# Masks, head products and the attention gate: two shared PSUM banks, and the gate's silu moved into attention

## The chip, the cores and the metric
The kernel runs on one core of a Trainium2 chip. TensorE (PE) does the matmuls into PSUM, of which there are eight banks of 128 x 512 float32; VectorE (DVE), ScalarE (ACT) and GpSimd (POOL) read and write SBUF and, but for POOL here, PSUM; SyncE (SP) issues the DMAs. Each engine runs its own instructions in order, and semaphores make one wait for another. The metric is the device time of one execution in microseconds; lower is better.

## The reference
An encoder layer over 1536 tokens: a prompt of 512 (seq0) and a sequence of 1024 (seq1). After a normed and modulated input, one in-projection feeds a latent attention branch and a bidirectional state space (SSD) branch, which are gated and projected out. What matters here is the SSD over chunks of 128 tokens, in 4 groups of 8 heads of width 64, both directions, and the attention's output gate:

```python
CB = einsum('bclgn,bcsgn->bcgls', Cc, Bc)            # one product of B and C per chunk and group
y_diag = einsum('bcgls,bcgels,bcsgep->bclgep', CB, Lm, xdt)   # Lm: decays, masked to one triangle
y_off  = einsum('bclgn,bcgepn,bclge->bclgep', Cc, prev, exp(a_cum))
y = y_diag + y_off + D * x                            # forward; the backward pass is summed to it
...
attn = softmax(q k^T) v * silu(gate_a)                # per head of 128
```

The exact form of the rest (norms, rotary part, convolution of width 5, projections) does not change.

## The kernel before
Tokens are worked on in windows of 512 (W), the SSD in chunks of 128 (P): 4 of seq0, 8 of seq1. A matmul of full precision is three products of split operands (mm3, L88 to L90). The stages follow one another: input and modulation to about 85 us, the four SSM groups to about 1600, attention to about 2190, then the output projections.

In each group g the convolution blocks of B, C and x come first, then `prepass` (the states of the backward direction, which are written out) and `mainpass` for seq0 and seq1. The program is written as generators: at every step of `mainpass` or `prepass` some blocks of the in-projection are fed in between as filler for PE (the 'mm' products). Groups 0 and 1 have the gate's eight blocks among their filler: two in group 0, six in group 1, three windows each. Their evacuation is a tanh on ACT (L524), (tanh + 1) times x on DVE (L525) and a store to `sgA` (L526). A scheduler places instructions by the program's order and its pools; semaphores are set by itself, and pools give out slots in turn.

`mainpass` takes a chunk in two halves of four heads (u = 0 and 1). By name: `head` (transposes through PSUM slots "sm", the copy `xb`, the product of B and C at L651 and its two masked forms `cu` at L653 and L654), `distances` (the load of `ab`), `weights` (POOL's differences L714, ACT's scaled masks `t` and `wt` at L718 and L719, DVE's sum L720, predicated copy L721, ACT's exponential L722), `weigh` (L727), `products` (four head matmuls into `py`, L738; the profile counts them in halves), `state` (`bth`, `btl`, `zt`: L688 to L691), `follow` (the new state, mm3 and DVE's `stf`), `carried` (what the old states give: matmuls L677 with `stf` and `sb`, DVE L678, sum L680) and `tail` (the sum of `py`, L743, and into x, L744). PSUM: three banks "mm" for the projections, three "sm" that transposes, the product of B and C, states and carried products share in turn, and two for `py`.

In attention a unit is one head and one window. `scores` makes the four blocks of scores and exponentials, `values` multiplies with v, and `gates` loads the gate `gt` (L1042), multiplies it by the softmax's reciprocal on POOL (L1043), and DVE applies it (L1072). 24 units; their steps are merged by weights, so that one unit's scores stand beside the one before's values.

Of the kernel before, what the change touches and what calls it, by code (L numbers as in the profile page):

```python
# [9 lines left out]
F32 = mybir.dt.float32  # L10
F32R = mybir.dt.float32r
U8 = mybir.dt.uint8
AF = mybir.ActivationFunctionType
ALU = mybir.AluOpType
AX = mybir.AxisListType
PSUM = bass.MemoryType.PSUM
DRAM = bass.MemoryType.DRAM

P = 128
T = 1536  # L20
W = 512
# [44 lines left out]
def _body(nc, tc, A, O):  # L66
    V, S, GP, PE = nc.vector, nc.scalar, nc.gpsimd, nc.tensor
    pools = []

    def pool(name, bufs=1, space=None, side="left"):  # L70
        cm = tc.tile_pool(name=name, bufs=bufs, side=side) if space is None else tc.tile_pool(name=name, bufs=bufs, space=space)
        p = cm.__enter__()
        pools.append((name, cm))
        return p
# [29 lines left out]
    cmat = const.tile([P, 5, P], F32, name="cmat")  # L104
    nc.sync.dma_start(out=cmat, in_=A["cmat"])
    maskb = const.tile([P, P], U8, name="maskb")
    ident, triF, triB, selL, selF = (cmat[:, i, :] for i in range(5))
# [153 lines left out]
    close("p0")  # L261


    yp = pool("yp", bufs=2, space=PSUM)
    p1 = pool("p1")
    pS = pool("pb", side="right")

# [246 lines left out]
    def filler(kind, i):  # L514
        if kind == "qc":
            def ev(w, ps):
                t = tmp("ft")
                S.copy(t, ps)
                nc.sync.dma_start(out=qcT[i][w], in_=t)
            return inproj_steps(i, ev)  # L520
        elif kind == "gate":
            def ev(w, ps):
                t = tmp("ft")
                S.activation(t, ps, AF.Tanh, scale=0.5)  # L524
                V.scalar_tensor_tensor(t, t, 1.0, ps, op0=ALU.add, op1=ALU.mult)  # L525
                nc.sync.dma_start(out=sgA[i][w], in_=t)  # L526
            return inproj_steps(BLK_GATE + i, ev)
        else:
            dst = tga if kind == "ga" else tgb

            def ev(w, ps):
                t = tmp("ft")
                S.activation(t, ps, AF.Tanh, scale=0.5)
                nc.sync.dma_start(out=dst[i][w], in_=t)
            return inproj_steps((BLK_GA if kind == "ga" else BLK_GB) + i, ev)
# [34 lines left out]
    for g in range(G):  # L570
# [61 lines left out]
        def mainpass(o, n):  # L632
# [5 lines left out]
            def head(c):  # L638
                cs_ = slice(c * P, (c + 1) * P)
                if c == c0:  # L640
                    xb = tok(c, "xb", 2)
                else:
                    xb = pS.tile([P, W + P], F32, name="xb", bufs=2)
                    nc.sync.dma_start(out=xb, in_=xbD[g][c])
                xt, bt = xb[:, :W], xb[:, W:]
                sb = None
                if c < c1 - 1:
                    sb = pS.tile([P, W], F32, name="sb", bufs=2)
                    nc.sync.dma_start(out=sb, in_=sbD[g][c])
                pc = smp.tile([P, P], F32, name="sm")  # L650
                PE.matmul(pc, lhsT=Bt[:, cs_], rhs=Ct[:, cs_], start=True, stop=True)  # L651
                cu = pS.tile([P, 2, P], F32, name="cu", bufs=2)
                V.tensor_tensor(cu[:, 0, :], pc, triF, op=ALU.mult)  # L653
                V.tensor_tensor(cu[:, 1, :], pc, triB, op=ALU.mult)  # L654
                stt[c] = dict(xt=xt, bt=bt, sb=sb, cu=cu)

            def decays(c):
                eb = {}
# [35 lines left out]
            def follow(c):  # L694
                stt[c]["sf"] = sf[0]
                if c < c1 - 1:
                    ps = smp.tile([P, W], F32, name="sm")
                    mm3(ps, *stt[c]["parts"], True, True)
                    sf[0] = advance(sf[0], ps, 0, c, pS.tile([P, W], F32, name="stf", bufs=2))
# [25 lines left out]
            def weigh(c, u):  # L725
                ab, wt = stt[c, u]
                V.tensor_tensor(wt, ab[:, 0], wt, op=ALU.mult)  # L727
                stt[c, u] = wt

            def products(c, u):  # L730
                e0 = u * HH
                wt = stt.pop((c, u))
                if u == 0:
                    stt[c]["py"] = yp.tile([P, 4, P], F32, name="py")
                py = stt[c]["py"]
                for e in range(e0, e0 + HH):
                    j = e % 2
                    PE.matmul(py[j * 64:j * 64 + 64, e // 2, :], lhsT=stt[c]["xt"][:, e * 64:e * 64 + 64], rhs=wt[:, e - e0, :], start=True, stop=True)  # L738

            def tail(c):  # L740
                cs_ = slice(c * P, (c + 1) * P)
                off = stt[c]["off"]
                V.tensor_tensor(off, off, stt[c]["py"], op=ALU.add)  # L743
                V.tensor_tensor(xa[:, :, cs_], xa[:, :, cs_], off, op=ALU.add)  # L744

            nu = E // HH
            us = [(c, u) for c in range(c0, c1) for u in range(nu)]
            head(c0)
            for i in range(4):
                xo = xs[i][:, o:o + n]  # L750
# [3 lines left out]
            weights(*us[0])  # L754
            yield
            for i in range(len(us) + 1):
                if i < len(us):
                    weigh(*us[i])
                if i + 2 < len(us):
                    distances(*us[i + 2])  # L760
                if i >= 1:
                    products(*us[i - 1])
                if i < len(us) and us[i][1] == 1:
                    follow(us[i][0])
                    carried(us[i][0])
                if i >= 1 and us[i - 1][1] == nu - 1:
                    tail(us[i - 1][0])
                if i + 1 < len(us):
                    weights(*us[i + 1])
                if i < len(us) and us[i][1] == 0:  # L770
                    c = us[i][0]
                    state(c)
                    decays(c)
                    if c + 1 < c1:
                        head(c + 1)
                yield
# [194 lines left out]
    def scores(u):  # L971
# [31 lines left out]
        def block(b):  # L1003
# [21 lines left out]
                S.activation(pp[k], sps[k], AF.Exp, bias=sm[:, 2:3], scale=rq[:, b, h:h + 1], accum_out=st["su"][:, k, b:b + 1])  # L1025
            PT[u].append(pp)

        def gates():

            su = st["su"]  # L1030
            if nw == 2:
                V.tensor_tensor(su[:, 0], su[:, 0], su[:, 1], op=ALU.add)
            V.reciprocal(su[:, 0], su[:, 0])
            pt = spp.tile([4, P], F32, name="sp")
            PE.transpose(out=pt, in_=su[:, 0], identity=ident)
            rt = p2.tile([4, P], F32, name="rt", bufs=2)
            S.copy(rt, pt)
            nc.sync.dma_start(out=rsD[hd][o // W + w].rearrange("(b q) -> b q", b=4), in_=rt)
            rb = p2.tile([P, W], F32, name="rb", bufs=1)
            nc.sync.dma_start(out=rb, in_=rsD[hd][o // W + w].partition_broadcast(P))  # L1040
            gt = p2.tile([P, W], F32, name="gt", bufs=1)
            nc.sync.dma_start(out=gt, in_=sgA[hd][o // W + w])  # L1042
            GP.tensor_tensor(gt, gt, rb, op=ALU.mult)  # L1043
            GT[u] = gt

        GT[u] = gates
        return [turn_n, turn_r], [lambda b=b: block(b) for b in range(4)]

    def values(u):

# [217 lines left out]
```

## Time and profile before

| | |
|---|---|
| median of 3 runs | 2720.13 us (2719.35 to 2723.41) |
| the profiled execution | 2716.42 us, span 2714.4, 2.0 us around it |
| mean granted clock of PE | 0.985 of full speed |
| busy: PE, DVE, ACT, POOL | 2586.5, 1833.5, 1322.6, 505.1 us |
| busy share of the same | 95%, 68%, 49%, 19% |

The busy share of PE is an average over stages with different limits; what holds a stage up is read from the waits and the timeline of that stage. A row of the waits says which tile's instruction waited, and the last operation that it waited for. A timeline row carries the idle time of its engine just ahead of it, with the releaser, in brackets. [...]

### The profile page before, as it was taken

What the parts mean: (1) busy time and instruction counts of PE and PEld (TensorE: products, weight loads), DVE (VectorE), ACT (ScalarE), POOL (GpSimd) and SP (SyncE); (2) the same over time, 40 slices, a digit from 0 to 9 for tenths busy, and PEclk for the clock granted to TensorE, in tenths of its full rate; (3) what the DMA queues carried; (4) which work ended last, traced back from release to release, by engine and by line L of the source; (5) the groups of instructions that cost most, each with busy time, mean ns of one, the idle gap of its engine ahead of it and who ended that gap; (6) DMA issues with size and microseconds to landing.
All of it is one profiled execution on the core that took longest, in us unless ns stands there. A gap on an engine that the chain in (4) does not pass through costs nothing. (4 is left out here: it accounts for less than half of the span.)

```text
span 2714.4 us, 36314 instructions
## 1 busy us (share of the span) xinstructions
PE 2586.5 (95%) x12810; PEld 2080.5 (77%) x12810; DVE 1833.5 (68%) x2962; ACT 1322.6 (49%) x2954; POOL 505.1 (19%) x455
## 2 busy tenths in 40 slices
PE   6999999999999998999998999999999999999999
PEld 2776777877778766878766888888888788888887
DVE  5878785788946678557777568877777753466631
ACT  5545654456624456564556357666665651111210
POOL 1013440023400035110135024322222200000000
PEclk8999999999999999999999999999999999999999
DMA  7227662156722266542466322211110252255433
GB/s 249 77 78 208 187 168 94 39 179 187 207 62 86 82 208 183 136 147 74 146 191 188 92 96 87 84 44 43 34 40 28 71 186 70 78 156 163 128 125 101
DMA packets 211205, 325.86 MB, mean 120 GB/s; under 512 B 24816, under 2 KB 74064, under 8 KB 210256
## 3 DMA queue, kind: packets, MB, share of 16 engines
q1 hardware_dynamic: 211024, 323.55, 39.9%
q8 instruction: 101, 1.65, 0.3%
q14 instruction: 80, 0.66, 0.1%
HBM read 245.56 MB, written 77.91 MB: 119 GB/s over the span
## 5 line engine op out<-in xcount | busy, mean ns | idle before, releaser
L88 PE MATMUL mm<-hH,wh 128*128 128x512 f32 x1656 | 670.2, 405 | 2.3 <-ACT hH L218 2.0
L89 PE MATMUL mm<-hL,wh 128*128 128x512 f32 x1656 | 662.0, 400 | 3.6 <-DVE hL L219 3.6
L90 PE MATMUL mm<-hH,wl 128*128 128x512 f32 x1656 | 653.7, 395 | 1.3 <-DVE wl L85 1.2
L88 PEld LDWEIGHTS mm<-hH,wh 128*128 128x128 f32 x1656 | 314.6, 190 | 84.6 <-issue 14.6
L89 PEld LDWEIGHTS mm<-hL,wh 128*128 128x128 f32 x1656 | 315.4, 190 | 77.3 <-issue 10.2
L90 PEld LDWEIGHTS mm<-hH,wl 128*128 128x128 f32 x1656 | 314.6, 190 | 73.2 <-issue 6.1
L714 POOL TENSOR_TENSOR ab<-ab,dg 128x512 f32<-128x512 f32 x192 | 236.9, 1246 | 418.5 <-DMA ab<-arD 293.4
L88 PE MATMUL mm<-hi,wh 128*128 128x512 f32 x768 | 298.8, 389 | 0.0
L90 PE MATMUL mm<-hi,wl 128*128 128x512 f32 x768 | 298.8, 389 | 0.0
L89 PE MATMUL mm<-lo,wh 128*128 128x512 f32 x768 | 298.8, 389 | 0.0
L85 DVE TENSOR_TENSOR wl<-ws,wh 128x512 fp32r<-128x512 f32 x210 | 151.3, 722 | 134.4 <-ACT wh L226 86.7
L361 ACT CAST wh<-ws 128x512 fp32r<-128x512 f32 x72 | 44.9, 623 | 326.4 <-PE mm L89 311.3
L88 PEld LDWEIGHTS mm<-hi,wh 128*128 128x128 f32 x768 | 144.1, 188 | 30.1
L89 PEld LDWEIGHTS mm<-lo,wh 128*128 128x128 f32 x768 | 144.1, 188 | 29.9
L90 PEld LDWEIGHTS mm<-hi,wl 128*128 128x128 f32 x768 | 144.1, 188 | 29.9
L719 ACT ACTIVATE wt<-cu,dg 128x128 f32<-128x128 f32 x384 | 141.3, 391 | 46.5 <-DVE cu L653 46.1
L1025 ACT ACTIVATE pp<-sp,smx,rq 128x512 f32<-128x512 f32 x160 | 123.6, 777 | 54.9 <-DVE smx L1020 38.8
L361 ACT CAST ph<-tp 128x512 fp32r<-128x512 f32 x160 | 95.3, 598 | 110.4 <-PE tp L1059 110.2
L689 POOL TENSOR_TENSOR btl<-xb,bth 128x128 fp32r<-128x128 f32 x40 | 28.5, 713 | 607.5 <-ACT bth L688 607.4
L563 DVE SCALAR_TENSOR_TENSOR xs<-raw,cwh,xs 128x511 f32<-128x511 f32 (+3 forms) x128 | 129.7, 1021 | 17.5 <-ACT xs L559 14.8
L718 ACT ACTIVATE t<-cu,dg 128x128 f32<-128x128 f32 x384 | 137.3, 390 | 2.6 <-DVE cu L654 2.4
L721 DVE COPY_PREDICATED ab<-maskb,ab 128x512 f32<-128x512 uint8 x96 | 86.4, 905 | 69.3 <-POOL ab L714 69.3
(293 smaller groups left out, 5018.5 us busy)
## 6 DMA issues: line engine op xcount, KB each, us to landing
ab<-arD SPq DMA_DIRECT2D x192, 256.0 KB
ws<-w_in SPq DMA_DIRECT2D x140, 256.0 KB
eb<-arD SPq DMA_DIRECT2D x160, 128.0 KB
xbD<-xp SPq DMA_DIRECT2D x40, 320.0 KB
xb<-xbD SPq DMA_DIRECT2D x40, 320.0 KB
yT<-xs SPq DMA_DIRECT2D x48, 256.0 KB
sg<-yT SPq DMA_DIRECT2D x48, 256.0 KB
tg<-tga SPq DMA_DIRECT2D x48, 256.0 KB
```

The source lines that it names most:

```text
L85: V.tensor_tensor(out, a, b, op=ALU.subtract)
L88: PE.matmul(out, lhsT=ah, rhs=bh, start=first, stop=False)
L89: PE.matmul(out, lhsT=ah, rhs=bl, start=False, stop=False)
L90: PE.matmul(out, lhsT=al, rhs=bh, start=False, stop=last)
L361: S.copy(hi, src)
L563: V.scalar_tensor_tensor(acc[:, lo:hi], raw[:, lo + d:hi + d], cwh[:, 24 + 24 * k + tix:24 + 24 * k + tix + 1], acc[:, lo:hi], op0=ALU.mul ...
L689: GP.tensor_tensor(bl, stt[c]["bt"], r32(bh), op=ALU.subtract)
L714: GP.tensor_tensor(ab[:, d], ab[:, d], ac_[:, d, c, e0:e0 + HH].unsqueeze(2).broadcast_to([P, HH, P]), op=ALU.subtract)
L718: S.activation(t1[:, e], cu[:, 1, :], AF.Copy, scale=dt_[:, 1, c, e0 + e:e0 + e + 1])
L719: S.activation(wt[:, e], cu[:, 0, :], AF.Copy, scale=dt_[:, 0, c, e0 + e:e0 + e + 1])
L721: V.copy_predicated(ab[:, 0], maskb.unsqueeze(1).broadcast_to([P, HH, P]), ab[:, 1])
L1025: S.activation(pp[k], sps[k], AF.Exp, bias=sm[:, 2:3], scale=rq[:, b, h:h + 1], accum_out=st["su"][:, k, b:b + 1])
```

## The change
The product of B and C gets a bank of its own (`pcb`), in which chunk c writes quarter c mod 4, and is made by a function `masks` one chunk ahead, at the start of a chunk; both masked forms are one DVE operation of 128 x 256. The heads' products of both halves get one bank (`pyb`) for all chunks; each half is summed into the carried part by a function `total` of its own, straight behind the carried products, and `tail` keeps only the sum into x. `state` stands at the start of a chunk's first half, ahead of `weigh`. The gate's evacuation becomes a plain copy, and tanh (ACT) and two products (POOL) go to attention, into a step `silu` behind the four score blocks of each unit; the gate has three buffers, the tanh one.

```diff
--- before.py
+++ after.py
@@ -261,7 +261,9 @@
     close("p0")
 
 
-    yp = pool("yp", bufs=2, space=PSUM)
+    yp = pool("yp", space=PSUM)
+    pyb = yp.tile([P, 4, P], F32, name="py")
+    pcb = yp.tile([P, 4, P], F32, name="pc")
     p1 = pool("p1")
     pS = pool("pb", side="right")
 
@@ -521,8 +523,7 @@
         elif kind == "gate":
             def ev(w, ps):
                 t = tmp("ft")
-                S.activation(t, ps, AF.Tanh, scale=0.5)
-                V.scalar_tensor_tensor(t, t, 1.0, ps, op0=ALU.add, op1=ALU.mult)
+                S.copy(t, ps)
                 nc.sync.dma_start(out=sgA[i][w], in_=t)
             return inproj_steps(BLK_GATE + i, ev)
         else:
@@ -647,12 +648,16 @@
                 if c < c1 - 1:
                     sb = pS.tile([P, W], F32, name="sb", bufs=2)
                     nc.sync.dma_start(out=sb, in_=sbD[g][c])
-                pc = smp.tile([P, P], F32, name="sm")
+                stt[c] = dict(xt=xt, bt=bt, sb=sb, cu=stt[c])
+
+            def masks(c):
+
+                cs_ = slice(c * P, (c + 1) * P)
+                pc = pcb[:, c % 4, :]
                 PE.matmul(pc, lhsT=Bt[:, cs_], rhs=Ct[:, cs_], start=True, stop=True)
                 cu = pS.tile([P, 2, P], F32, name="cu", bufs=2)
-                V.tensor_tensor(cu[:, 0, :], pc, triF, op=ALU.mult)
-                V.tensor_tensor(cu[:, 1, :], pc, triB, op=ALU.mult)
-                stt[c] = dict(xt=xt, bt=bt, sb=sb, cu=cu)
+                V.tensor_tensor(cu, pc.unsqueeze(1).broadcast_to([P, 2, P]), cmat[:, 1:3, :], op=ALU.mult)
+                stt[c] = cu
 
             def decays(c):
                 eb = {}
@@ -730,21 +735,21 @@
             def products(c, u):
                 e0 = u * HH
                 wt = stt.pop((c, u))
-                if u == 0:
-                    stt[c]["py"] = yp.tile([P, 4, P], F32, name="py")
-                py = stt[c]["py"]
                 for e in range(e0, e0 + HH):
                     j = e % 2
-                    PE.matmul(py[j * 64:j * 64 + 64, e // 2, :], lhsT=stt[c]["xt"][:, e * 64:e * 64 + 64], rhs=wt[:, e - e0, :], start=True, stop=True)
+                    PE.matmul(pyb[j * 64:j * 64 + 64, e // 2, :], lhsT=stt[c]["xt"][:, e * 64:e * 64 + 64], rhs=wt[:, e - e0, :], start=True, stop=True)
+
+            def total(c, u):
+                off = stt[c]["off"][:, 2 * u:2 * u + 2, :]
+                V.tensor_tensor(off, off, pyb[:, 2 * u:2 * u + 2, :], op=ALU.add)
 
             def tail(c):
                 cs_ = slice(c * P, (c + 1) * P)
-                off = stt[c]["off"]
-                V.tensor_tensor(off, off, stt[c]["py"], op=ALU.add)
-                V.tensor_tensor(xa[:, :, cs_], xa[:, :, cs_], off, op=ALU.add)
+                V.tensor_tensor(xa[:, :, cs_], xa[:, :, cs_], stt[c]["off"], op=ALU.add)
 
             nu = E // HH
             us = [(c, u) for c in range(c0, c1) for u in range(nu)]
+            masks(c0)
             head(c0)
             for i in range(4):
                 xo = xs[i][:, o:o + n]
@@ -754,22 +759,28 @@
             weights(*us[0])
             yield
             for i in range(len(us) + 1):
+                c, u = us[min(i, len(us) - 1)]
+                begins = i < len(us) and u == 0
+                if begins:
+                    if c + 1 < c1:
+                        masks(c + 1)
+                    state(c)
                 if i < len(us):
-                    weigh(*us[i])
+                    weigh(c, u)
                 if i + 2 < len(us):
                     distances(*us[i + 2])
                 if i >= 1:
                     products(*us[i - 1])
-                if i < len(us) and us[i][1] == 1:
-                    follow(us[i][0])
-                    carried(us[i][0])
+                if i < len(us) and u == 1:
+                    follow(c)
+                    carried(c)
+                if i >= 1:
+                    total(*us[i - 1])
                 if i >= 1 and us[i - 1][1] == nu - 1:
                     tail(us[i - 1][0])
                 if i + 1 < len(us):
                     weights(*us[i + 1])
-                if i < len(us) and us[i][1] == 0:
-                    c = us[i][0]
-                    state(c)
+                if begins:
                     decays(c)
                     if c + 1 < c1:
                         head(c + 1)
@@ -1025,6 +1036,15 @@
                 S.activation(pp[k], sps[k], AF.Exp, bias=sm[:, 2:3], scale=rq[:, b, h:h + 1], accum_out=st["su"][:, k, b:b + 1])
             PT[u].append(pp)
 
+        def silu():
+
+            gt = st["gt"] = p2.tile([P, W], F32, name="gt", bufs=3)
+            nc.sync.dma_start(out=gt, in_=sgA[hd][o // W + w])
+            tg = p2.tile([P, W], F32, name="tgt", bufs=1)
+            S.activation(tg, gt, AF.Tanh, scale=0.5)
+            GP.tensor_tensor(tg, tg, gt, op=ALU.mult)
+            GP.tensor_tensor(gt, tg, gt, op=ALU.add)
+
         def gates():
 
             su = st["su"]
@@ -1038,13 +1058,12 @@
             nc.sync.dma_start(out=rsD[hd][o // W + w].rearrange("(b q) -> b q", b=4), in_=rt)
             rb = p2.tile([P, W], F32, name="rb", bufs=1)
             nc.sync.dma_start(out=rb, in_=rsD[hd][o // W + w].partition_broadcast(P))
-            gt = p2.tile([P, W], F32, name="gt", bufs=1)
-            nc.sync.dma_start(out=gt, in_=sgA[hd][o // W + w])
+            gt = st["gt"]
             GP.tensor_tensor(gt, gt, rb, op=ALU.mult)
             GT[u] = gt
 
         GT[u] = gates
-        return [turn_n, turn_r], [lambda b=b: block(b) for b in range(4)]
+        return [turn_n, turn_r], [lambda b=b: block(b) for b in range(4)] + [silu]
 
     def values(u):
```

What moves is shown at three places. PE at the long gap between two chunks of seq1 in the last group, before: the last half's products, the product of B and C (into `sm`), the next chunk's first products, the new state (zt, bth), and the carried products.

```order
L738 MATMUL py<-wt,xb 64x128 x3
L651 MATMUL sm<-ch,kd 128x128 [waits DVE_49]
L738 MATMUL py<-wt,xb 64x128 [waits DMAHW2_49,Activation_49]
L738 MATMUL py<-wt,xb 64x128 [waits Activation_49] x3
L88 MATMUL sm<-zt,bth 128x512 [waits DVE_49,Activation_49]
L89 MATMUL sm<-zt,bth 128x512 [waits Pool_49]
L90 MATMUL sm<-zt,btl 128x512
L677 MATMUL sm<-ch,stf 128x128 [waits DVE_49]
L677 MATMUL sm<-ch,stf 128x128 x3
L88 MATMUL mm<-hH_401,wh 128x512
L677 MATMUL sm<-ch,sb 128x128 [waits DMAHW1_49,DVE_49]
L677 MATMUL sm<-ch,sb 128x128 x3
```

And now (py and pc are the two banks):

```order
L657 MATMUL pc<-ch,kd 128x128
L740 MATMUL py<-wt,xb 64x128 [waits DVE_49]
L740 MATMUL py<-wt,xb 64x128
L740 MATMUL py<-wt,xb 64x128 [waits Activation_49] x2
L88 MATMUL sm<-zt,bth 128x512 [waits Activation_49]
L89 MATMUL sm<-zt,bth 128x512 [waits Pool_49]
L90 MATMUL sm<-zt,btl 128x512
L682 MATMUL sm<-ch,stf 128x128 [waits PE_49]
L682 MATMUL sm<-ch,stf 128x128
L740 MATMUL py<-wt,xb 64x128 [waits DMAHW6_49,DVE_49]
L740 MATMUL py<-wt,xb 64x128 x3
L682 MATMUL sm<-ch,stf 128x128 x2
```

The product of B and C has gone in front of the last half's products; the next chunk's products have gone behind the new state and half of the carried products with stf, and wait for DVE.

DVE at the same place, before: predicated copies, splits of a projection's weights (wl), the sum of py, the masks, the sum into x.

```order
L721 COPY_PREDICATED ab<-maskb,ab 128x512 [waits Pool_49]
L85 TENSOR_TENSOR wl<-ws,wh 128x512 [waits PE_49,Activation_49]
L721 COPY_PREDICATED ab<-maskb,ab 128x512 [waits Pool_49]
L85 TENSOR_TENSOR wl<-ws,wh 128x512 [waits DMAHW3_49,PE_49,Activation_49]
L743 TENSOR_TENSOR eb<-eb,py 128x512 [waits DVE_49,PE_49]
L653 TENSOR_TENSOR cu<-sm,cmat 128x128 [waits PE_49]
L744 TENSOR_TENSOR xs<-xs,eb 128x4x128 [waits DVE_49]
L654 TENSOR_TENSOR cu<-sm,cmat 128x128
L609 TENSOR_TENSOR stf<-stf,sm 128x512 [waits PE_49]
```

And now, with `total` as L744 and the masks as L659:

```order
L726 COPY_PREDICATED ab<-maskb,ab 128x512 [waits Pool_49]
L85 TENSOR_TENSOR wl<-ws,wh 128x512 [waits PE_49,Activation_49]
L726 COPY_PREDICATED ab<-maskb,ab 128x512 [waits Pool_49]
L659 TENSOR_TENSOR cu<-pc,cmat 128x256 [waits PE_49]
L85 TENSOR_TENSOR wl<-ws,wh 128x512 [waits DMAHW1_49,Activation_49]
L744 TENSOR_TENSOR eb<-eb,py 128x256 [waits PE_49]
L610 TENSOR_TENSOR stf<-stf,sm 128x512 [waits DVE_49,PE_49]
L748 TENSOR_TENSOR xs<-xs,eb 128x4x128 [waits DVE_49]
L683 TENSOR_TENSOR eb<-eb,sm 128x512 [waits DMAHW0_49,DMAHW7_49,PE_49,Activation_49]
```

The masks are one row, behind the second predicated copy, and the sum of py is half as wide; the sum into x (L748) stands behind the update of stf.

POOL at the same place, with buffer numbers since its rows are much alike; before, the pair of differences ab_12330, then btl and zt of the next chunk, then the pair ab_12380:

```order
L714 TENSOR_TENSOR ab_12330<-ab_12330,dg_10905 128x512 [waits DMAHW0_49,DVE_49,Pool_49]
L714 TENSOR_TENSOR ab_12330<-ab_12330,dg_10905 128x512 [waits DMAHW1_49]
L689 TENSOR_TENSOR btl_12357<-xb_12218,bth_12356 128x128 [waits DMAHW2_49,PE_49,Activation_49]
L691 TENSOR_TENSOR zt_12359<-tmp_12354,zt_12358 128x512 [waits Activation_49]
L714 TENSOR_TENSOR ab_12380<-ab_12380,dg_10905 128x512 [waits DMAHW3_49]
L714 TENSOR_TENSOR ab_12380<-ab_12380,dg_10905 128x512 [waits DMAHW4_49]
L714 TENSOR_TENSOR ab_12466<-ab_12466,dg_10905 128x512 [waits DMAHW0_49,DVE_49,Pool_49]
L714 TENSOR_TENSOR ab_12466<-ab_12466,dg_10905 128x512 [waits DMAHW1_49]
```

And now, where ab_12231 and ab_12266 are those pairs:

```order
L719 TENSOR_TENSOR ab_12231<-ab_12231,dg_10811 128x512 [waits DMAHW5_49,DVE_49,Pool_49]
L694 TENSOR_TENSOR btl_12223<-xb_12111,bth_12222 128x128 [waits DMAHW6_49,PE_49,Activation_49]
L696 TENSOR_TENSOR zt_12225<-tmp_12220,zt_12224 128x512 [waits Activation_49]
L719 TENSOR_TENSOR ab_12231<-ab_12231,dg_10811 128x512 [waits DMAHW2_49]
L719 TENSOR_TENSOR ab_12266<-ab_12266,dg_10811 128x512 [waits DMAHW3_49]
L719 TENSOR_TENSOR ab_12266<-ab_12266,dg_10811 128x512 [waits DMAHW5_49]
L719 TENSOR_TENSOR ab_12365<-ab_12365,dg_10811 128x512 [waits DMAHW6_49,DVE_49,Pool_49]
L719 TENSOR_TENSOR ab_12365<-ab_12365,dg_10811 128x512 [waits DMAHW1_49]
```

btl and zt have moved between the two halves of the first pair.

At the start of attention three tanh now stand on ACT among the weight splits (wqh, wkh) and the evacuations of the first q blocks (qrw, sq): one ahead of the first block's, one behind it and one behind the second's. The second and the third wait for POOL, which multiplies out of the same buffer.

## Rows read from the trace of the kernel before
**Rows 1.** The page's part 1: busy time of each engine, share, instructions
```profile
PE 2586.5 (95%) x12810; PEld 2080.5 (77%) x12810; DVE 1833.5 (68%) x2962; ACT 1322.6 (49%) x2954; POOL 505.1 (19%) x455
```

**Rows 2.** PE's waits, whole run: line, waited for, us in total, times, longest
```profile
PE sm L677 <- DVE cu L654: 21.8, 7, 4.8
...
PE sm L89 <- POOL zt L691: 14.3, 10, 3.2
...
PE po L89 <- DVE pl L85: 5.2, 6, 0.9
...
PE sm L651 <- ACT xb L592: 4.8, 3, 2.1
...
PE sm L651 <- DVE stf L609: 1.9, 3, 0.7
```

**Rows 3.** Timeline of PE, long gap: start, duration, operation, idle before, releaser
```profile
1457.65 0.80 PE L89 MATMUL sm<-zt,bth 128*128 128x512 f32 x1 [3.10 <-POOL zt L691]
...
1464.87 2.08 PE L677 MATMUL sm<-ch,sb 128*128 128x128 f32 x8 [3.90 <-DVE cu L654]
```

**Rows 4.** Timeline of POOL, long gap
```profile
1451.72 3.79 POOL L714 TENSOR_TENSOR ab<-ab,dg 128x512 f32<-128x512 f32 x2 [6.62 <-DMA ab<-arD]
1455.47 0.45 POOL L689 TENSOR_TENSOR btl<-xb,bth 128x128 fp32r<-128x128 f32 x1
1455.88 1.72 POOL L691 TENSOR_TENSOR zt<-tmp,zt 128x512 fp32r<-128x512 f32 x1
1457.56 2.48 POOL L714 TENSOR_TENSOR ab<-ab,dg 128x512 f32<-128x512 f32 x2
```

**Rows 5.** Timeline of DVE, long gap
```profile
1460.07 0.73 DVE L721 COPY_PREDICATED ab<-maskb,ab 128x512 f32<-128x512 uint8 x1 [1.93 <-POOL ab L714]
1462.07 1.15 DVE L85 TENSOR_TENSOR wl<-ws,wh 128x512 fp32r<-128x512 f32 x1 [1.26 <-ACT wh L226]
1463.14 0.68 DVE L743 TENSOR_TENSOR eb<-eb,py 128x512 f32<-128x512 f32 x1
...
1464.53 0.28 DVE L654 TENSOR_TENSOR cu<-sm,cmat 128x128 f32<-128x128 f32 x1
```

**Rows 6.** Timeline of PE, short gap
```profile
1414.00 0.66 PE L738 MATMUL py<-wt,xb 128*64 128x128 f32 x8
...
1416.53 0.50 PE L89 MATMUL sm<-zt,bth 128*128 128x512 f32 x1 [1.43 <-POOL zt L691]
...
1417.09 1.05 PE L677 MATMUL sm<-ch,stf 128*128 128x128 f32 x8
1420.21 1.16 PE L677 MATMUL sm<-ch,sb 128*128 128x128 f32 x8 [2.07 <-DVE cu L654]
```

**Rows 7.** Timeline of DVE, short gap
```profile
1411.30 0.67 DVE L720 TENSOR_TENSOR wt<-wt,t 128x512 f32<-128x512 f32 x1
...
1415.28 1.74 DVE L720 TENSOR_TENSOR wt<-wt,t 128x512 f32<-128x512 f32 x1
...
1417.73 0.68 DVE L743 TENSOR_TENSOR eb<-eb,py 128x512 f32<-128x512 f32 x1
```

**Rows 8.** Busy by stretch: PE, PEld, DVE, ACT, POOL; clock, DMA share, GB/s
```profile
1396.00:1500.00 104.00, 90.79 (x496) 71.97 (x496) 81.44 (x123) 67.82 (x188) 48.18 (x40) 0.95 0.62 172
```

**Rows 9.** Groups, 220 to 1510 us: count, busy, mean ns, idle before
```profile
L88 PE MATMUL mm<-hH,wh 128*128 128x512 f32 x1339 | 542.7, 405 | 0.2 <-ACT wh L226 0.2
...
L525 DVE SCALAR_TENSOR_TENSOR ft<-ft,mm 128x512 f32<-128x512 f32 x24 | 16.3, 680 | 4.2 <-ACT ft L524 4.2
...
L524 ACT ACTIVATE ft<-mm 128x512 f32<-128x512 f32 x24 | 14.1, 587 | 10.6 <-PE mm L90 10.5
```

**Rows 10.** Timeline of ACT, start of attention
```profile
1607.51 0.36 ACT L879 COPY qrw<-sp 128x256 f32<-128x256 f32 x1
```

**Rows 11.** Timeline of POOL, start of attention
```profile
1612.24 1.31 POOL L898 TENSOR_TENSOR qrr<-qy,qx 128x512 f32<-128x512 f32 x1 [4.30 <-DVE ssq L894]
```

**Rows 12.** Groups of POOL, attention (1600 to 2190 us)
```profile
L1043 POOL TENSOR_TENSOR gt<-gt,rb 128x512 f32<-128x512 f32 x24 | 31.0, 1293 | 257.0 <-DMA rb<-rsD 217.0 <-DVE smx L1020 16.1 <-DVE qx L889 12.0
```

## Prediction
> **What bounds the kernel now.** I read the page's busy shares first: TensorE is busy for 2586.5 us, 95% of the span [rows 1], so a change can only win in what is left, some 128 us, or in the clock. The second view is the list of PE's waits. Four of its rows lie in the SSM groups, at matmuls that this change moves or whose PSUM slot it changes: the carried products wait for the second mask product of B and C (21.8 us, 7 times), the new state's second product waits for POOL's zt (14.3 us), the product of B and C itself waits for a slot, through the copy xb (4.8) and through stf (1.9). Together 42.8 us [rows 2]. PE's wait for DVE's pl, in attention, is told of in part 6.
>
> The third view is the timeline of PE in the last group, seq1. The waits are not spread out: two places of each group hold most of them, where the two products of neighbouring chunks stand without filler between them. In the last group the later place (I call it the long gap) stalls 3.10 and 3.90 us [rows 3]; the earlier (the short gap) 1.43 and 2.07 [rows 6]. What ends last there is read from POOL and DVE. POOL does the pair for the distances L714, btl, zt and the next pair without a pause from 1451.72 to 1460.04 [rows 4]; DVE's predicated copy starts behind it at 1460.07, wl at 1462.07, the head's sum L743 at 1463.14, and the second mask product at 1464.53 to 1464.81 [rows 5]; PE goes on at 1464.87. So the long gap is paced by a chain POOL, DVE, PE, not by PSUM alone. [...]
>
> **The change part by part.** The sum is made against the profiled execution, 2716.4 us (span 2714.4 and 2.0 around it); the median of the runs shown is 3.7 above it, and I add that at the end.
>
> 1. Masks out of the shared PSUM slots. The product of B and C no longer takes one of three "sm" slots, so its own waits for xb and stf (6.7 us) go, and carried products no longer wait for the masks. At most 6.7; what takes their place at the start of a chunk is the transposes' slots, so from 0 to −6.7. I take −6, since the quarter it writes now is long free there.
>
> 2. The two gaps. In the new order PE has in the long gap: first products, new state, half of the carried stf quad, then the next products, which wait for the sum `total` of the first half. DVE has in front of that sum the same predicated copy, the masks as one operation and wl. On POOL, btl and zt now stand between the halves of a distance pair. The pair took 3.79 us where the next took 2.48 [rows 4], so its second half came late, and btl and zt fall into that hole: zt ends at 1451.72 + 1.24 + 0.45 + 1.72 = 1455.1 instead of 1457.6, the next pair at 1455.1 + 1.24 + 2.48 = 1458.8 instead of 1460.0. On DVE then: copy 0.73, wl 2.0 behind the copy's start as before and 1.15 long, `total` about 0.33 (half of the 0.68 of L743) [rows 5]: done at about 1462.3, PE at 1462.4, 2.5 earlier. But behind the wait there now stand the products (0.66), half of the stf quad (half of 1.05 [rows 6]) and a filler matmul (0.4 [rows 9]) that lay in front of it. Left: about 0.9 us. In the short gap the sum ends about where L743 does, 1418.3, (1417.73 and 0.68 less a little [rows 7]), where PE was released at 1420.2 [rows 6], and 1.8 − 0.66 − 0.53 leaves about 0.6. Both gaps, four groups: 4 × 1.5 = −6. Bounds: +8, if zt and the copy stay where they are and only the added matmuls count (4 × 2 × 1.0); −36, if both waits (21.8 and 14.3) go.
>
> 3. New waits. Every quad of products now waits for the sum before it. Most have 7 to 24 filler matmuls (0.4 us each [rows 9]) in front, more than DVE needs. Without filler stand the two gaps, the last pair of seq1 (three stf matmuls between), and two pairs in seq0. The last three, four groups: 12 places. Nothing of before shows this wait. Between 0 and 2.07 us each [rows 6]; I take 0.7, between the row of L743 (0.68) and nothing hidden: +8; ends 0 and +25.
>
> 4. DVE's gate product. L525 runs 24 times, 16.3 us busy, all in the first two groups [rows 9], and goes; the masks become one operation and the sum two halves, which is even. A third of it lay on DVE's path to PE by the share of such stretches that PE loses to it: −5, from 0 to −15. ACT keeps one pass there, a copy for the tanh.
>
> 5. Clock. [...] 5% of a stretch of 104 us is 5 us a group [rows 8]; I take a fifth, −4, from 0 to −20.
>
> [...]
>
> 6. Attention. Tanh and the two products of the gate go there: 24 tanh on ACT (0.59 each, the row of L524 [rows 9]) and 48 POOL products of 1.29 us, the row of L1043 [rows 12]: 62 us more on POOL, beside PE. At the start it is dear: three tanh share one buffer, so the second waits until POOL is through with the first, and ACT is in order. POOL is busy until 1607.9, the start of qrr at 1612.24 less the 4.30 it was idle [rows 11]; the two products end at about 1610.5; the ACT copies behind, of which the first began at 1607.51 [rows 10], come 3 to 5 us later, and with them the key weights for PE. I take 4, from 0 to 8. POOL's qrr has those 4.30 us of room. For the 24 units I take 0.15 each, 4, from 0 to 20: the wait of po for pl is 5.2 us now [rows 2] and grows if POOL slows DVE. That POOL does so is seen at the short gap: the sum L720 takes 0.67 alone and 1.74 beside zt [rows 7].
>
> [...]
>
> Sum: −6 −6 +8 −5 −4 +4 +4 = −5; 2716.4 − 5 = 2711.4, and 3.7 to the median: about 2715 us.
>
> **The rivals.**
> A. The one bank sets the end (slower). At the 20 pairs without filler (five in each group) the products wait for a sum that stands behind predicated copy and wl on DVE. For it: rows 5 show DVE 2 to 3 us behind there. Against: the sum now stands ahead of xs and of the second mask. At 1.0 us at each of 20 pairs, nothing won at the gaps, and the slots' 6, +20 − 6 + 8 = +22, and 3.7 to the median: 2742 us. With nothing won at the gaps it decides from about 0.2 us at each pair on (20 × 0.2 − 6 + 8 + 3.7 is 2726).
> B. The gate costs more in attention: ACT waits at each of the 24 units for POOL or for the gate's load, 0.6 each, and 7 at the start: 21 in place of 8: 2728 us. For it: one buffer for the tanh and an in-order ACT that also releases PE's exp and ph. Against: ACT is busy for 49% of the span [rows 1].
> C. The waits are only renamed: the chain POOL, DVE sets the pace of both gaps, the slots' 6 us come back at the next gap, and new and old waits are even; gates win 4, attention costs 4: 2716.4 + 3.7, about 2720 us, no change. For it: rows 4 and 5, which show a chain without PSUM in it.
> D. All four waits go, with 8 us of clock: −43 − 8 + 8 + 8 (new waits, attention) = −35: 2685 us. Against: the chain in rows 4 and 5 has still to be run.
>
> **How the numbers follow.** A measurement can tell 0.2%, 5.4 us, from no change: faster is under 2714.7, slower over 2725.6. Forecast 0.46 (its own range 2705 to 2725: 0.26 faster, 0.20 same), D 0.12 (faster), C 0.17 (0.04 faster, 0.10 same, 0.03 slower), A 0.15 and B 0.10 (slower). Faster 0.42, same 0.30, slower 0.28. The range 2693 to 2735 leaves out most of D and of A, together under 0.2.
>
> **What would show it.** In PE's waits: no wait of carried products for the masks; a new one of the products for `total`, 1 to 5 us at each gap; the waits for xb and stf at the mask product gone; zt below 10 us. DVE without L525; the granted clock in the last group's 104 us at 0.95 or a little more; ACT waiting for POOL at the start of attention for some 3 us, twice; attention longer by about 8 us. I am wrong if waits for `total` also stand at pairs with filler in front, if attention pays over 15 us, or if zt goes altogether.

## The result: slower, by 0.83 to 1.16%

The changed kernel takes 2743.89 us (median of 4 runs, 2740.75 to 2749.1) against 2719.74 us before in the same comparison; the ratio is 1.010 (95% interval 1.0083 to 1.0116). The forecast was 2715 in a range of 2693 to 2735. The profiled execution took 2749.1 us with a span of 2747.1, so 32.7 us more than that of before: PE is busy for some 8.5 us more and idle for some 24 us more. It is the slowest of the four runs; the medians are 24.2 us apart.

The page's part 1 of the kernel after [rows 1], and PE's waits in the four groups (220 to 1560 us), columns as in [rows 2]:

```profile
PE 2595.1 (94%) x12810; PEld 2093.2 (76%) x12810; DVE 1835.0 (67%) x2938; ACT 1341.8 (49%) x2978; POOL 564.3 (21%) x503
```
```profile
PE py L740 <- DVE eb L744: 62.8, 30, 6.1
PE sm L627 <- DVE eb L683: 10.7, 4, 3.2
PE sm L591 <- DVE eb L683: 5.8, 4, 1.9
PE py L740 <- DVE wt L732: 5.1, 4, 2.1
```

All four rows on which the forecast stood are gone: no wait for the masks, for zt, or of the product of B and C for its slot, 42.8 us before [rows 2]. In their place stands one row, the heads' products waiting for DVE's sum of the half before: 62.8 us. That is 20 more. Where they lie in the last group, seq1 (timeline of PE, the rows with that wait):

```profile
1445.10 0.80 PE L740 MATMUL py<-wt,xb 128*64 128x128 f32 x8 [2.48 <-DVE eb L744]
...
1460.65 1.12 PE L740 MATMUL py<-wt,xb 128*64 128x128 f32 x8 [4.46 <-DVE eb L744]
...
1487.81 0.66 PE L740 MATMUL py<-wt,xb 128*64 128x128 f32 x8 [1.16 <-DVE eb L744]
...
1493.61 1.12 PE L740 MATMUL py<-wt,xb 128*64 128x128 f32 x8 [3.80 <-DVE eb L744]
```

1445.10 is the short gap (before: 1.43 and 2.07 [rows 6]) and 1493.61 the long one (before: 3.10 and 3.90 [rows 3]). 1460.65 is new, and it is the place that the prediction left out: products of a second half, with 31 filler matmuls ahead of them. The first and the last two of those:

```profile
1448.41 0.70 PE L88 MATMUL mm<-hH,wh 128*128 128x512 f32 x1
...
1455.56 0.39 PE L90 MATMUL mm<-hH,wl 128*128 128x512 f32 x1
1455.79 0.40 PE L88 MATMUL mm<-hH,wh 128*128 128x512 f32 x1
```

The rows are 0.4 us long, but overlap: they start 0.23 us apart. So 31 of them cover 7.8 us, to 1456.19, and not 31 times 0.4, which is 12.4. DVE just there:

```profile
1456.32 0.67 DVE L683 TENSOR_TENSOR eb<-eb,sm 128x512 f32<-128x512 f32 x1
1456.91 1.48 DVE L85 TENSOR_TENSOR wl<-ws,wh 128x512 fp32r<-128x512 f32 x1
1458.32 1.52 DVE L685 TENSOR_TENSOR eb<-eb 128x512 f32<-128x512 f32 x1
1459.76 0.41 DVE L659 TENSOR_TENSOR cu<-pc,cmat 128x256 f32<-128x256 f32 x1
1460.10 0.41 DVE L744 TENSOR_TENSOR eb<-eb,py 128x256 f32<-128x256 f32 x1
```

The first half's products had long been made. But their sum goes into the carried part, and that is ready only after L683 and L685; until the sum has been read out, the second half's products wait. So the carried chain, which had a whole chunk's time before, now stands between the two halves of a chunk, together with what lies around it in DVE's queue (wl, the masks). The four groups have this wait at 322, 688, 1071 and 1461 us: 3.23, 3.97, 4.07 and 4.46, together 15.7.

At the gaps it is another thing. There the next chunk's first products wait for the sum of the last chunk's second half, whose carried part is long done. DVE at the long gap:

```profile
1485.30 0.68 DVE L685 TENSOR_TENSOR eb<-eb 128x512 f32<-128x512 f32 x1
...
1487.67 1.24 DVE L726 COPY_PREDICATED ab<-maskb,ab 128x512 f32<-128x512 uint8 x1
1488.81 1.51 DVE L85 TENSOR_TENSOR wl<-ws,wh 128x512 fp32r<-128x512 f32 x1
1490.25 1.56 DVE L726 COPY_PREDICATED ab<-maskb,ab 128x512 f32<-128x512 uint8 x1
1491.71 0.40 DVE L659 TENSOR_TENSOR cu<-pc,cmat 128x256 f32<-128x256 f32 x1
1492.03 1.18 DVE L85 TENSOR_TENSOR wl<-ws,wh 128x512 fp32r<-128x512 f32 x1
1493.14 0.41 DVE L744 TENSOR_TENSOR eb<-eb,py 128x256 f32<-128x256 f32 x1
```

The carried part ended at 1485.98 and the products at 1488.47; the sum stands behind two predicated copies, two wl and the masks. In two of the four groups the copies in turn wait for POOL's differences there (2.05 and 0.93 us in the first, 0.60 and 0.93 in the third). The short gaps have 14.8 and the long gaps 18.8, together 33.6, where masks and zt had 34.6 of their 36.1 before. 18 smaller waits make 13.5, of which 8.8 at 11 places with 12 to 24 filler matmuls in front.

The granted clock in the last group fell from 0.95 to 0.92 [rows 8]:

```profile
1420.00:1530.00 110.00, 94.20 (x508) 75.74 (x506) 90.14 (x126) 69.03 (x188) 48.05 (x40) 0.92 0.61 166
```

And the start of attention, ACT:

```profile
1640.66 0.63 ACT L1044 ACTIVATE tgt<-gt 128x512 f32<-128x512 f32 x1 [3.68 <-POOL gt L1046]
...
1644.07 0.63 ACT L1044 ACTIVATE tgt<-gt 128x512 f32<-128x512 f32 x1 [1.47 <-POOL gt L1046]
```

From ACT's first evacuation there (1601.42 before, 1631.49 after) to the end of the span it is 1113.0 us before and 1115.6 after. So of the 32.7 us all but 3 were lost in the groups. Up to those two times PE is busy for 0.4 us more and idle for 29.7 us more: the lower clock cost nothing there that can be seen, and the loss is waiting. Behind them PE is busy for 8.1 us more and idle for 5.5 us less; in the first 100 us of attention the granted clock is 0.97, where it was 1.00.

### The profile page after: what moved, and what is told of

It is laid out like the page before. It is cut to its first block, busy times and chain, and to the rows that moved or that the text cites. A ratio compares the mean times of both kernels' runs of the same rounds, so it can differ in the third digit from the quotient of the medians.

```text
span 2747.1 us, 36378 instructions
## 1 busy us (share of the span) xinstructions
PE 2595.1 (94%) x12810; PEld 2093.2 (76%) x12810; DVE 1835.0 (67%) x2938; ACT 1341.8 (49%) x2978; POOL 564.3 (21%) x503
## 4 chain that ended last, share of the span: by engine, by line
PE 70%; DVE 11%; DMA 7%; ACT 4%; issue 3%; POOL 2%; SPq 0%; DVEq 0%; ACTq 0%; POOLq 0%
PE mm L90 16%; PE mm L89 16%; PE mm L88 16%; DMA ab<-arD 3%; PE tp L1078 2%; PE sp L90 1%; PE sp L89 1%; PE sp L88 1%; POOL ab L719 1%; DMA eb<-arD 1%; PE sp L1023 1%; PE sp L1024 1%; PE sp L1025 1%; PE sp L1026 1%; PE po L88 1%
## 5 line engine op out<-in xcount | busy, mean ns | idle before, releaser
L363 ACT CAST wh<-ws 128x512 fp32r<-128x512 f32 x72 | 44.8, 622 | 326.6 <-PE mm L89 312.5
L723 ACT ACTIVATE t<-cu,dg 128x128 f32<-128x128 f32 x384 | 139.7, 394 | 33.0 <-DVE cu L659 30.0
L226 ACT CAST wh<-ws 128x512 fp32r<-128x512 f32 x138 | 84.4, 616 | 114.4 <-PE mm L89 109.0
```

Of the source, the lines that this page charges most:

```text
L226: S.copy(a, ws)
L723: S.activation(t1[:, e], cu[:, 1, :], AF.Copy, scale=dt_[:, 1, c, e0 + e:e0 + e + 1])
```

## The experiments

Ratios are to the kernel before, run beside it on the same chip; 0.1% is 2.7 us.

**First four: one part at a time.** e1, a bank for each half, the product of B and C in the first half's free quarters:

```diff
-    pyb = yp.tile([P, 4, P], F32, name="py")
-    pcb = yp.tile([P, 4, P], F32, name="pc")
+    pyb = [yp.tile([P, 4, P], F32, name=f"py{u}") for u in range(2)]
...
+                pc = pyb[0][:, 2 + c % 2, :]
```

> The changed kernel with one PSUM bank for the products of the first half and one for those of the second; the product of B and C writes the two quarters left free in the first half's bank. Order of the program, early state and gate as in the changed kernel. Theory 'one bank' (the 62.8 us in which products wait for the sum of the half before are lost because both halves share a bank, and that sum stands behind the carried chain on DVE): that wait falls below 15 us, and the time to 2705 to 2722. Theory 'order' (early state, early masks and the filler that they move set the pace through POOL and DVE; the wait for the sum is only where it is seen): the wait is renamed, to masks, zt or wt, and the time stays at 2735 to 2748.

2742.51 us, 1.0093 (1.0074 to 1.0112): by its time, for 'order', and a miss for 'one bank'. But its waits say that I had only moved the sharing:

```profile
PE py L656 <- DVE eb L743: 27.6, 14, 4.8
PE py L739 <- DVE cu L658: 22.4, 8, 4.1
```

The product of B and C now waits for the first half's sum, since it writes the same bank, and the next products wait for DVE's reading of the product there, to make the masks. The run told nothing between the theories.

e2, the gate alone (`silu` and the plain copy put into the kernel before):

> The kernel before with the gate's tanh and products moved into attention, and nothing else. Theory 'one bank': the gate costs about 2 us in attention and gives up to 5 in the first two groups: 2714 to 2724. Theory 'gate' (the move spoils attention or the filler): over 2728.

2722.55 us, 1.0021 (1.0008 to 1.0035): some 6 us dearer, inside the first range, though nothing of the gain that it had counted on in the first two groups is seen.

e3, the changed order with the PSUM of before (`yp` with two buffers, one a chunk; `pc` in `smp`):

> The changed kernel with the PSUM of before: products of a chunk in one of two banks in turn, the product of B and C in one of the three shared slots; early state, early masks, sums by halves and the gate as changed. Theory 'one bank': no wait of products for a sum, 2705 to 2722. Theory 'order': 2735 to 2748.

2736.79 us, 1.0079 (1.0058 to 1.0099): a miss for 'one bank' as I had put it, and in the range of 'order'. Yet the wait is that of the changed kernel:

```profile
PE py L741 <- DVE eb L745: 49.8, 27, 5.2
```

Halves of a chunk still share a bank, and are summed apart. From this comes the sharper theory 'halves'.

e4, the kernel before with `yp` at one buffer:

> The kernel before with one bank for the products in place of two (eight quads of a chunk, one sum at its end), and nothing else. Theory 'one bank': products of the next chunk wait for the sum of this one, at the two gaps and the last pair of each group: 12 to 20 waits of 2 to 4 us, 2740 to 2765. Theory 'order': the bank alone costs under 8 us, 2718 to 2727.

2726.27 us, 1.0032 (1.0017 to 1.0046): in the range of 'order', if a little over its 8 us by the ratio (8.7), and far under that of 'one bank'. The waits came in the number that 'one bank' had, in place of those for the masks, 21.8 us before:

```profile
PE py L738 <- DVE eb L743: 34.6, 14, 5.2
```

**Second four: halves or order.** e5 is e3 with one sum a chunk, e6 the changed kernel with one sum a chunk:

```diff
-                if i >= 1:
-                    total(*us[i - 1])
                 if i >= 1 and us[i - 1][1] == nu - 1:
+                    total(us[i - 1][0])
                     tail(us[i - 1][0])
```

> The kernel e3_order_only (order and gate of the changed kernel, PSUM of before) with one sum per chunk at its end in place of two sums by halves. Theory 'halves' (what costs is that the second half's products wait for the first half's sum, which stands on DVE behind the chunk's carried chain, while both halves are in one bank): the waits of products for a sum fall from 49.8 us to under 10, and the time from 2737 to 2714 to 2726. Theory 'order' (early state and early masks are themselves worse): it stays at 2732 to 2742.

2733.3 us, 1.0062 (1.0046 to 1.0078): in the range of 'order'. The waits for sums went, and the time didn't. Waits of the product of B and C for a shared slot, behind stf, and for the masks took their place:

```profile
PE sm L655 <- DVE stf L608: 24.2, 6, 7.4
PE sm L680 <- DVE cu L657: 14.7, 7, 4.0
```

A miss for 'halves' alone.

> The changed kernel with its two banks kept, and one sum per chunk in place of two by halves. Theory 'halves': one wait a chunk is left, that of the next chunk's products for the sum, as in e4_one_bank: 2724 to 2736. Theory 'order': 2738 to 2748.

2737.41 us, 1.0074 (1.0057 to 1.0092): 7 us under the changed kernel by the ratios, between the two ranges. With halves summed together, products still wait for a sum, that of the whole chunk before:

```profile
PE py L740 <- DVE eb L744: 48.7, 14, 7.1
```

So one bank for successive chunks holds PE up by itself, with the larger part of the wait at the long gaps.

e7, sums by halves in the kernel before, in a chunk's bank:

> The kernel before with the sum made by halves, the first behind the carried products, and nothing else: a chunk's bank, order, masks and gate as before. Theory 'halves': products of the second half wait for the sum of the first, 25 to 50 us in all; 2724 to 2738. Theory 'order': 2711 to 2722.

2729.52 us, 1.0045 (1.0030 to 1.0060):

```profile
PE py L738 <- DVE eb L742: 31.7, 24, 4.4
```

'Halves' holds in the old order. e4 and e7 together are 0.77% of the changed kernel's 1.0%; that the two simply add is not shown.

e8, e1 with `pc` back in a shared slot, so that no two of these share a bank; order, sums by halves and gate as changed:

```diff
-                pc = pyb[0][:, 2 + c % 2, :]
+                pc = smp.tile([P, P], F32, name="sm")
```

> The kernel e1_half_banks with the product of B and C moved out of the first half's bank into a shared slot: halves summed apart, each in a bank of its own, order and gate as changed. Theory 'halves': each half's products wait for a sum half a chunk old, under 10 us in all; 2712 to 2726. Theory 'order': 2734 to 2746.

2719.17 us, 1.0010 (0.9998 to 1.0022): the changed order with other banks is 0.9% faster than the changed kernel, and products wait for a sum for 1.8 us in all. 'Order' falls.

**Third four: with and without the gate.** e9 gives each half and the product of B and C a bank, the last from the projections; e10 and e11 are e9 and e8 with the gate of before, e12 the changed kernel with the gate of before.

```diff
-    mmp = pool("mmp", bufs=3, space=PSUM)
+    mmp = pool("mmp", bufs=2, space=PSUM)
...
+    pcb = yp.tile([P, 4, P], F32, name="pc")
```

> The changed kernel (order, sums by halves, gate) with a bank for each half's products and one for the product of B and C; the bank for it is taken from the projections, which keep two of three. Theory 'banks' (what costs is only that DVE's reads and PE's writes meet in one bank; the order itself gains): the 15.8 us that the product of B and C waits for a shared slot in e8_half_banks_sm go: 2704 to 2717. Rival 'filler' (two projection banks make PE wait for their evacuation, which stands in ACT's and DVE's queues): 2722 to 2740, with new waits at the mm products.

2718.3 us, 1.0007 (0.9997 to 1.0017).

> e9_three_banks with the gate's tanh and product back at the evacuation, as in the kernel before. If the gate's move costs what e2_gate_only shows (6 us), 6 us under e9; 2698 to 2712 by the theory 'banks'. If its cost depends on the order around it: within 2 us of e9.

2716.94 us, 0.9999 (0.9986 to 1.0011), within 2 us of e9. Both lie some us over the range of 'banks' and under that of 'filler': the wait for the slot is gone, and nothing was won by it. The largest row of PE's waits in both is now at the heads' products, and the profile shows no releaser for it ("issue"); e9, then e10:

```profile
PE py L740 <- issue: 21.5, 8, 5.1
PE py L741 <- issue: 20.4, 12, 4.7
```

What ends these waits is open.

> e8_half_banks_sm with the gate back as in the kernel before. Gate additive: 2719 less 6, 2710 to 2716, a little under the kernel before. Not additive: 2717 to 2722.

2716.36 us, 0.9999 (0.9986 to 1.0012): between its two ranges, and not under the kernel before, where the first of them had it.

> The changed kernel with the gate back as in the kernel before; banks and order as changed. Gate additive: 2744 less 6, 2734 to 2741. If the gate's move takes load off DVE in the first two groups where the new waits for the sums are: 2744 to 2752.

2735.95 us, 1.0065 (1.0046 to 1.0083), in the first range.

e11 and e12 differ in the banks alone, 2716.36 against 2735.95: sharing costs 18 us by the ratios, 19.6 by the medians. With the moved gate (e8 against the changed kernel) it is 0.9%, 24 us. The gate's move costs 9, 6, 3 and 2 us by the ratios of four pairs (the changed kernel and e12, e2 and the kernel before, e8 and e11, e9 and e10), each known to some 4 to 7 us: a few us. Whether it is more where PE waits anyway, the intervals leave open. And no kernel of these gains on the one before.

**Fourth four: why nothing is gained.** e13 has the old order and gate with the banks of e9, and sums by halves; e14 is the kernel before with `pcb` and two projection banks; e15 is e5 with the same; e16 is the kernel before with two projection banks.

> The kernel before (its order, masks in two operations, state late, gate as before) with the banks of e10: one for each half's products, summed apart, one for the product of B and C, and two projection banks. Theory 'chain' (with PSUM free the gaps are set by loads, POOL and DVE, whatever the order): 2711 to 2720, within 4 us of e10's 2717. Theory 'order gains' (early state and masks are worth 10 us or more once no bank is shared): 2724 to 2732.

2715.92 us, 1.0001 (0.9989 to 1.0012): in the range of 'chain'.

> The kernel before with the product of B and C in a bank of its own, taken from the projections' three, and nothing else. Theory 'slots' (the waits of carried products for the masks, 21.8 us, and of the product of B and C for its slot, 6.7 us, are PSUM's): 2690 to 2705. Theory 'chain' (they are renamed: PE comes to the next wait on the same chain): 2711 to 2720.

2716.01 us, 0.9997 (0.9981 to 1.0012): in the range of 'chain' too.

> e5_order_one_sum (new order and gate, a bank a chunk, one sum a chunk) with the product of B and C in a bank of its own, taken from the projections. If the shared slot is what makes e5 slow (24.2 us behind stf): from 2733 to 2716 to 2723. If it is the one sum a chunk in this order: 2729 to 2736.

2722.29 us, 1.0021 (1.0007 to 1.0035), in the first range: the shared slot was most of what made e5 slow. The same wait is 15.8 us in e8 and 24.2 us in e11, as much as in e5, and they are not slower than the kernel before; why is left open.

> The kernel before with two projection banks in place of three, and nothing else; it gives the price of the bank that e9, e10 and e13 to e15 take. If each block's 24 matmuls cover the evacuation: 2714 to 2720. If not: 2724 to 2740, with waits at the mm products.

2720.45 us, 1.0024 (1.0009 to 1.0038), just over the first range: the third projection bank is worth 4 us by the medians and 6.5 by the ratio, at waits for wl and raw that were small before.

So the own bank for the product of B and C is worth about as much (e14 against e16: 4 us by the medians, 7 by the ratios, known to some 6), and old and new order are even (e13, e10). PE's waits of e14 (220 to 1560 us) show where the 21.8 us for the masks went:

```profile
PE sm L89 <- POOL zt L693: 35.9, 19, 4.4
PE sm L628 <- DVE eb L680: 8.6, 4, 3.0
```

They became waits for POOL's zt, 35.9 for 14.3 [rows 2]. In e13 the new row is that without a releaser, 15.8 us at the heads' products.

**Last two: who ends last there.** e17 is e14, and e18 is e10, with the two residuals on DVE:

```diff
-                    GP.tensor_tensor(bl, stt[c]["bt"], r32(bh), op=ALU.subtract)
+                    sub(bl, stt[c]["bt"], r32(bh))
...
-                    GP.tensor_tensor(xl, xd, r32(xh), op=ALU.subtract)
+                    sub(xl, xd, r32(xh))
```

> e14_pc_bank with the two residuals btl and zt made on DVE in place of POOL: 40 each, on DVE some 0.68 and 0.3 us. Theory 'POOL ends last' (PE's 35.9 us behind POOL's zt is POOL's queue): 2690 to 2708. Theory 'DVE paces' (DVE is busy for nine tenths of these stretches; 39 us more on it take what POOL gives): 2711 to 2724, the wait for zt renamed to DVE's.

2696.0 us, 0.9924 (0.9907 to 0.9942).

> e10_three_banks_gate_back with btl and zt on DVE. Theory 'POOL ends last': 2704 to 2712 (PE's wait for zt is 7.5 us there, and POOL's differences come earlier). Theory 'DVE paces': 2714 to 2728.

2703.43 us, 0.9945 (0.9926 to 0.9964), slightly under its range.

Both times speak for 'POOL ends last' and against 'DVE paces', and e17 is faster than both kernels of this case. The edit does two things, though, and the runs don't part them: it takes btl and zt out of POOL's queue, and it takes POOL's work away from beside DVE's (last section). In e17 the wait for zt fell by 21.8 us and the time by 20; in e18 the time fell by 13.5 us, and the wait for zt had been only 7.5. Part 1 of the page of e14, then of e17, and e17's wait for zt:

```profile
PE 2580.9 (95%) x12810; PEld 2078.7 (77%) x12810; DVE 1840.3 (68%) x2962; ACT 1321.6 (49%) x2954; POOL 502.6 (19%) x455
```
```profile
PE 2577.0 (96%) x12810; PEld 2075.6 (77%) x12810; DVE 1842.7 (68%) x3042; ACT 1323.1 (49%) x2954; POOL 417.6 (16%) x375
```
```profile
PE sm L89 <- DVE zt L85: 14.1, 11, 3.2
```

## Why the prediction was wrong

- **The step that failed is 3, new waits.** It said that most quads "have 7 to 24 filler matmuls (0.4 us each [rows 9]) in front, more than DVE needs", and took 12 places without filler at 0.7 us, +8. Outside the gaps, which are step 2's, the trace has 22 waits with 29.2 us. The seven with no more than 4 filler matmuls in front make 4.7, less than the 8. The other 15, behind 12 to 31, were put at nothing and make 24.5, of which 15.7 at the four second halves.

  Two things were wrong there. Filler was priced too high: the matmuls start 0.23 us apart, so that 31 cover 7.8 us; at 0.4 they would have covered the 12.1 us from the first of them to the end of the sum. And I had priced the sum by its own length, and not by its other input, the carried part, which ends a chain of loads, ACT, PE and DVE. A bank shared by two halves ties the second half's products to that chain.

  e7 shows this cost by itself (0.45%), e4 that of one bank for successive chunks (0.32%), e8 and e11 that with other banks it is gone. That waits for `total` stand at pairs with filler in front, and that zt's wait is gone altogether, are two of the signs by which the prediction said that it would be wrong.
- **Rival A** named the right resource, and for the gaps the right mechanism: no filler, and a sum behind predicated copy and wl on DVE. Eight of the twelve large waits, 33.6 us, are of this kind. That its total, 2742 us, came out is in part luck: it had 20 pairs at 1.0 us each, where the gaps' waits, 2.5 to 6.1 us each, only take the place of those before, and most of what is added elsewhere, 24.5 of 29.2 us, stands behind filler.
- **Step 1** took −6 for the slots. The waits did go, but other small rows of PE's waits in the groups grew by some 9 us together, none by 3; e14 against e16 puts a bank for the product of B and C at −4 to −7, and e16 its price on the projections at about the same.
- **Step 2** had zt's wait gone or smaller, and it is; it left 0.9 and 0.6 us to win at the two gaps of a group. The gaps' waits went from 34.6 us to 33.6: 1.0 won in all four groups, where 6 were forecast, since the sum waits in DVE's queue as the masks did. The chain POOL, DVE, PE that it was read from was the right one: e14 renames the wait along it, and e17 shortens it. The consequence, to which I gave only 0.17, is rival C's: taking PSUM waits away in that chain gives little (e8 to e11, e13 and e14 are all within 0.1% of the kernel before).
- **Steps 4 and 5** were gains that did not come. The gate's product off DVE gave nothing that can be seen: e2 and e12 show the move as dearer by 6 and 9 us. The granted clock was 0.981 over the span, after 0.985, and PE's busy time in the groups was even (0.4 us more), where −4 was forecast. No run shows that −4. In the trace of before, read in steps of 1 us, the clock is 0.50 from 1458 to 1460 and from 1465 to 1471, behind PE's waits of 3.10 and 3.90 us [rows 3], and 1.00 behind the short gap's [rows 6]; the changed kernel has waits of that length too, 4.46 and 3.80 us in the last group, and 0.50 behind them, from 1460 to 1465 and from 1494 to 1496. No run shows by itself the third of L525's 16.3 us that step 4 put on DVE's path to PE. What the gate's move costs in the groups is open: in the single profiles about 10 us of e2's and e12's differences lie there, more than the interval of their times bears out.
- **Step 6** was right in kind: the second and third tanh hold ACT for 3.68 and 1.47 us behind POOL, forecast as 3 to 5 together. For the 24 units I took 4 us more; from there to the end the whole difference is 2.6 us, for both terms. The row of pl in attention after, 0.684 us each,

```profile
L85 DVE TENSOR_TENSOR pl<-tp,ph 128x512 fp32r<-128x512 f32 x160 | 109.0, 684 | 22.1 <-ACT ph L363 20.9
```

stands against 0.686 before, with 60 us more on POOL: pl, which has one input in PSUM, was not slowed. Nor was the sum L743 in the kernel before, which has one input in PSUM as well: 0.668 to 0.689 us in all 48, of which 22 stand beside POOL's work for more than half of their length.

## What to carry to other kernels

Before two producers share a PSUM bank, follow the reader that frees it through all of its inputs and through its engine's queue: an addition into something that is still being made holds the bank as long as that takes (here the products waited up to 4.46 us for it, behind 31 filler matmuls). Take the length of filler from the starts of its rows (0.23 us apart here) and not from their durations (0.4 us), which overlap. When a wait is taken away, look for what is next on the same chain, and test it by the engine that ends last there: three arrangements of banks without the shared-bank waits came back to the old time, and moving 80 small operations off POOL then gave 0.7% (e17 against e14). An experiment that undoes sharing must be read by its waits first; e1 had put it back elsewhere.

## What was not expected of the hardware

DVE did 80 more operations in e17 and was busy for only 2.4 us more. Part of what paid for them is seen in the groups of DVE (220 to 1560 us), e14 and then e17; both operations have two inputs in SBUF:

```profile
L729 DVE TENSOR_TENSOR wt<-ab,wt 128x512 f32<-128x512 f32 x95 | 88.6, 933 | 0.9
L722 DVE TENSOR_TENSOR wt<-wt,t 128x512 f32<-128x512 f32 x94 | 81.5, 867 | 10.5 <-ACT wt L721 10.4
```
```profile
L729 DVE TENSOR_TENSOR wt<-ab,wt 128x512 f32<-128x512 f32 x95 | 74.5, 784 | 0.5
L722 DVE TENSOR_TENSOR wt<-wt,t 128x512 f32<-128x512 f32 x94 | 74.3, 790 | 13.4 <-ACT wt L721 13.1
```

0.933 and 0.867 us a piece became 0.784 and 0.790 with 85 us less on POOL; it is the difference between 0.67 alone and 1.74 beside POOL at the short gap [rows 7], here as a mean. These two rows give back 21.3 us; the copies L723, wl and the sums into x (L746) gave back another 12.2 (81.4, 89.5 and 42.3 us in e14, 76.6, 85.6 and 38.8 in e17). On POOL zt and btl had taken 59.7 and 29.1 us in that window of e14. So in these runs such operations were shorter with less of POOL's work beside them, and moving it to DVE was nearly free (2.4 us).
